# Zero-filled operands in a macaron block's attention and state-space stages: matmuls of 64 and 16 rows become matmuls of 128 rows

## The chip, the cores and the metric

One core of a Trainium2 chip runs the whole kernel. TensorE (PE) multiplies, with its weight loads shown apart (PEld); VectorE (DVE), ScalarE (ACT) and GpSimd (POOL) work beside it, and SyncE (SP) issues the weight transfers. The metric is the device time of one execution in microseconds, the median of three runs.

## The reference, cut to what matters

One layer, float32, with 16 learned meta tokens ahead of 256 positions (272 in all) and a model width of 2048:

```python
h = h + 0.5 * _swiglu(_rmsnorm(h, ffn1_norm), w_gate, w_up, w_down)      # 5632 wide
u = _rmsnorm(h, mix_norm) @ w_in                                        # q, k, v, z, x/B/C, dt
# group A: 8 heads of differential attention, two halves of 64 per head
s = einsum('bqhsd,bkhsd->bhsqk', q, k) * 64 ** -0.5;  p = softmax(where(mask, s, -inf))
w = p[:, :, 0] - lam * p[:, :, 1];  attn = rmsnorm(einsum('bhqk,bkhv->bqhv', w, v))
# group B: 16 heads of a chunked state-space scan (SSD), head size 64, state 128
h = h + concat(attn, ssd * silu(z) normed) @ w_out
h = h + 0.5 * _swiglu(_rmsnorm(h, ffn2_norm), ...);  return h[:, 16:]
```

Before the scores, q and k pass an RMS norm per half head and a rotation of the first 16 of the 64 dimensions.

## The kernel before, in words

Activations stand transposed: model dimension on the 128 partitions, positions along the row. Every weight tile (128 x 1024 float32, 512 KB) is loaded by SP, split into a high part by ACT (`hi`, L154) and a low rest by DVE (`lo`, L156), and multiplied two or three times on PE (`mm3`, L197 to L199, 272 columns; `mm2`, L204 and L205, 512 and 256 columns). These main matmuls take 128 rows and 128 columns of the array. `project` makes 4 blocks of 128 output rows from 8 weight tiles, into four of the five PSUM accumulators (`acc`); the next `project` starts in the fifth and then needs the first three of the previous one emptied.

Everything else is background work: `later(cost, fn)` puts a closure in a queue, and `step()`, called once per weight tile, runs closures worth 1.5 credits. So small float32 matmuls stand between the main ones on PE. A float32 matmul is two PE instructions (two passes); a transpose is one. The framework's scheduler fixes the final order on each engine when the program is built; at run time each engine works in order and waits on semaphores.

The matmuls that the change touches:

- `scores(h, j)`, L772: for head h and query block j, two products, one for each half s of the head. The half's 64 dimensions are rows 0 to 63 or 64 to 127 of `qT` and `kT`, so each takes 64 rows of the array; 144 columns for j = 0, 272 for j = 1. There are 16 pairs. DVE (L775 to L777), ACT (L779, L784) and DVE again (L781 to L785) make the softmax and the difference.
- `turn(h, j)`, L794 to L797: transposes the weights `w` and copies them to `wt0` or `wt1`; of the last block 16 rows are real.
- `values(h)`, L827 to L831: five products, of 128, 16, 128, 128 and 16 rows (L828 and L831 are those of 16).
- `ssd_mm(c)`, L652: for each of 8 head pairs three products per head of 128, 128 and 16 rows, 64 output rows each; the two heads of a pair take the left and the right 64 columns of the array.

Around them: `qk_evac` empties the accumulators of k (wi = 1) and q (wi = 0). For q, `join` (L226 on ACT, L227 on DVE) adds the two halves of the accumulator straight into `qT`; then ACT squares it (L676) into a row buffer and DVE scales it by the norm's weight (L677). Row buffers (`row_tmp`, tile name `t`) are 8 in all. The squares are summed by `qk_stat` (L686 on PE) in the background. `rope_in` and `rope` rotate by way of DRAM, with transfers issued by POOL (L704 to L720). `k_rows` (L745 to L755) sends k's norm factors through DRAM (`k_d`) and spreads them over the partitions; `k_scale` (L759, DVE) multiplies `kT` by them. Big activations (`qT`, `kT`, `V`, `Xd`, `O`, ...) are slots of one pool of 14 (tile name `u`).

Of the kernel before, what the change touches and what calls it, by code (L numbers as in the profile page):

```python
# [17 lines left out]
P = 128  # L18
# [66 lines left out]
def hymba_block(ctx: ExitStack, tc: tile.TileContext, h0, pars, consts, dtw, wts, out):  # L85
# [172 lines left out]
    def pc(i):  # L258
        return pcol[:, i:i + 1]
# [205 lines left out]

    brow = cp.tile([P, T], F32, name="brow")
    bcol = cp.tile([P, 3, P], F32, name="bcol")
    ends = [META - 1 + CHUNK * i for i in range(5)]

    def dt_1():  # L470
# [122 lines left out]


    Xd = Lazy([P, 1024])

    def x_step(c):
        ps = ps_tile()
# [26 lines left out]
    def ssd_exp(c):  # L625

        for h in (2 * c, 2 * c + 1):
            A = st["A"][h // 4][:, h % 4, :]

            def b(i, n, ch):  # L630
                return bcol[0:n, i, 32 * (ch - 1) + h:32 * (ch - 1) + h + 1]

            e = tmp("se", [P, 416], 4)
            for i, n, ch, o, l, k in ((0, P, 1, 0, 0, 64), (0, P, 2, 64, 64, 64), (1, P, 2, 256, 112, 16),
                                      (1, P, 3, 272, 128, 64), (1, P, 4, 336, 192, 64), (2, 16, 4, 400, 240, 16)):
                nc.vector.tensor_scalar(e[0:n, o:o + k], A[0:n, l:l + k], b(i, n, ch), 0.0, ALU.add, ALU.min)
            for ch in (3, 4):
                l = (ch - 1) * CHUNK
                nc.scalar.activation(e[:, l:l + CHUNK], A[:, l:l + CHUNK], AF.Exp, bias=b(0, P, ch))
            nc.scalar.activation(e[:, 0:P], e[:, 0:P], AF.Exp)  # L640
            nc.scalar.activation(e[:, 256:400], e[:, 256:400], AF.Exp)
            nc.scalar.activation(e[0:16, 400:416], e[0:16, 400:416], AF.Exp)
            nc.vector.tensor_tensor(e[:, 0:400], e[:, 0:400], S[h // 8][:, 0:400], ALU.mult)
            nc.vector.tensor_tensor(e[0:16, 400:416], e[0:16, 400:416], S[h // 8][0:16, 400:416], ALU.mult)
            es[h] = e

    def ssd_mm(c):
        py = ps_tile()
        for i, n, o, l in ((0, P, 0, 0), (1, P, 256, 112), (2, 16, 400, 240)):
            for j in range(2):  # L650
                h = 2 * c + j
                nc.tensor.matmul(py[j * 64:(j + 1) * 64, l:SEQ], Xd[i][0:n, h * 64:(h + 1) * 64],  # L652
                                 es[h][0:n, o:o + SEQ - l], start=i == 0, stop=i == 2)
        y = xs[c // 4][:, c % 4, META:T]
        nc.vector.scalar_tensor_tensor(y, y, dsk[:, c:c + 1], py[:, 0:SEQ], ALU.mult, ALU.add)
# [5 lines left out]
    later(0.1, lambda: (load_A(0), load_A(1)))  # L661


    kT, qT = Lazy([P, 4, T]), Lazy([P, 4, SEQ])

    def qk_evac(pj, g, dst, wi):

        sqs = []
        if wi == 0:
            for c in range(4):  # L670
                join(dst[g][:, c, :], pj[c])
            pj = [dst[g][:, c, :] for c in range(4)]
        for c in range(4):
            p = pj[c]
            sq = row_tmp(p.shape[1])
            nc.scalar.activation(sq, p, AF.Square)  # L676
            nc.vector.tensor_scalar(dst[g][:, c, :], p, pc(R_QN + wi), None, ALU.mult)  # L677
            sqs.append(sq)
        return sqs

# [18 lines left out]
    def rope_in(dst, g, n):  # L699

        d = dp.tile([2, ROT, 4, T], F32, name=nm("rope"))
        a = row_tmp(n)
        for half in range(2):
            nc.gpsimd.dma_start(d[half][:, :, 0:n], dst[g][half * HD:half * HD + ROT, :, :])  # L704
        for half in range(2):
            nc.gpsimd.dma_start(a[half * HD:(half + 1) * HD, :],
                                d[half].rearrange("r c t -> c r t")[:, :, 0:n])
        return a

    def rope(a, dst, g, t0):  # L710
        n = T - t0
        b_ = row_tmp(n)
        nc.vector.stream_shuffle(b_, a, shuf)
        nc.vector.tensor_tensor(b_, b_, sin_t[:, t0:T], ALU.mult)
        nc.vector.tensor_tensor(a, a, cos_t[:, t0:T], ALU.mult)
        nc.vector.tensor_tensor(a, a, b_, ALU.add)
        d = dp.tile([P, T], F32, name=nm("roped"))
        nc.gpsimd.dma_start(d[:, 0:n], a)
        for half in range(2):
            nc.gpsimd.dma_start(dst[g][half * HD:half * HD + ROT, :, :],  # L720
                                d[half * HD:(half + 1) * HD, 0:n].rearrange("(c r) t -> r c t", c=4))

    kst, qst = cp.tile([P, 3, 16], F32, name="kst"), cp.tile([P, 2, 16], F32, name="qst")
# [40 lines left out]
    def scores(h, j):  # L764

        kw = 144 if j == 0 else T
        w = tmp("sw", [P, 2, T], 3)
        mx, sm = tmp("mx", [P, 2]), tmp("sm", [P, 2], 3)
        pss = [ps_tile()[:, 0:kw] for _ in range(2)]
        for s in range(2):  # L770
            r = slice(s * HD, (s + 1) * HD)
            nc.tensor.matmul(pss[s], qT[h // 4][r, h % 4, j * P:(j + 1) * P], kT[h // 4][r, h % 4, 0:kw],  # L772
                             start=True, stop=True)
        for s in range(2):
            nc.vector.memset(pss[s][0:64, kw - 64:kw], -1e30)  # L775
            nc.vector.reduce_max(mx[:, s:s + 1], pss[s], axis=AX.X)
        nc.vector.scalar_tensor_tensor(mx, mx, -1.0, rq[:, j, 2 * h:2 * h + 2], ALU.mult, ALU.mult)  # L777
        for s in range(2):
            nc.scalar.activation(w[:, s, 0:kw], pss[s], AF.Exp, bias=mx[:, s:s + 1],  # L779
                                 scale=rq[:, j, 2 * h + s:2 * h + s + 1], accum_out=sm[:, s:s + 1])  # L780
        nc.vector.reciprocal(sm, sm)  # L781
        nc.vector.tensor_tensor(sm[:, 0:1], sm[:, 0:1], il, ALU.mult)
        nc.vector.tensor_tensor(sm[:, 1:2], sm[:, 1:2], nlam, ALU.mult)
        nc.scalar.activation(w[:, 1, 0:kw], w[:, 1, 0:kw], AF.Copy, scale=sm[:, 1:2])  # L784
        nc.vector.scalar_tensor_tensor(w[:, 0, 0:kw], w[:, 0, 0:kw], sm[:, 0:1], w[:, 1, 0:kw], ALU.mult, ALU.add)  # L785
        ws[h, j] = w

    def turn(h, j):
        w = ws.pop((h, j))
        pt = ps_tile()  # L790
        n = 1 + j
        t = tmp(f"wt{j}", [P, 256 + P * j])
        for i in range(n):
            nc.tensor.transpose(pt[:, i * P:(i + 1) * P], w[:, 0, i * P:(i + 1) * P], ident)  # L794
        nc.tensor.transpose(pt[0:16, n * P:(n + 1) * P], w[:, 0, n * P:n * P + 16], ident)
        nc.scalar.copy(t[:, 0:n * P], pt[:, 0:n * P])
        nc.scalar.copy(t[0:16, n * P:(n + 1) * P], pt[0:16, n * P:(n + 1) * P])  # L797
        wT[h, j] = t

    V = Lazy([P, 1024])  # L800

    def v_copy(pj):
        ts = []
# [19 lines left out]
    def values(h):  # L823
        ps = ps_tile()
        v = slice(h * P, (h + 1) * P)
        t0, t1 = wT.pop((h, 0)), wT.pop((h, 1))
        nc.tensor.matmul(ps[:, 0:P], t0[:, 0:P], V[0][:, v], start=True, stop=False)  # L827
        nc.tensor.matmul(ps[:, 0:P], t0[0:16, P:2 * P], V[1][0:16, v], start=False, stop=True)  # L828
        nc.tensor.matmul(ps[:, P:2 * P], t1[:, 0:P], V[0][:, v], start=True, stop=False)
        nc.tensor.matmul(ps[:, P:2 * P], t1[:, P:2 * P], V[1][:, v], start=False, stop=False)  # L830
        nc.tensor.matmul(ps[:, P:2 * P], t1[0:16, 2 * P:3 * P], V[2][0:16, v], start=False, stop=True)  # L831
        g, c = h // 4, h % 4
        for j in range(2):
            sq = row_tmp(P)
            nc.scalar.activation(sq, ps[:, j * P:(j + 1) * P], AF.Square, accum_out=osq[:, g, j, c:c + 1])
        nc.scalar.copy(O[g][:, :, c, :], ps[:, 0:2 * P].rearrange("p (j v) -> p j v", j=2))
# [76 lines left out]
    for c in range(8):  # L913
        later(1.2, z_b, c, label=f"z{c}")
    nc.vector.memset(kst, 1.0)
    for dst, stat, spans, t0, wi in ((kT, kst, TT, 0, 1), (qT, qst, ZT, META, 0)):
        for g in range(2):
            pj = project(t0)
            sqs = qk_evac(pj, g, dst, wi)
            a = rope_in(dst, g, T - t0)  # L920
            later(1.0, nop)
            later(0.7, lambda sqs=sqs, g=g, spans=spans, stat=stat: later_first(0.7, qk_turn, qk_stat(sqs), g, spans, stat))
            later(1.5, rope, a, dst, g, t0)
        if t0 == 0:
            later(1.0, k_rstd)
            later(0.3, nop)
            later(0.7, k_rows)
            later(1.2, k_scale, 0)
            later(1.2, k_scale, 1)
        else:  # L930
            later(1.0, head_rstd, qst, rq, (3, 4), HD ** -0.5)
    for g in range(2):
        pj = project(0)
        need("z7")
        ts = v_copy(pj)
        for c in range(4):
            later(0.0, v_turn, ts[c], 4 * g + c)
# [178 lines left out]
```

## Time and profile before

| | us |
|---|---|
| median of 3 runs (lowest, highest) | 1972.01 (1971.01, 1973.12) |
| the profiled execution's own time | 1974.47 |
| its span, first to last instruction | 1972.7 |
| granted TensorE clock over the span, share of full | 0.999 |
| PE busy / PEld / DVE / ACT / POOL | 1960.8 / 1804.7 / 1142.3 / 927.3 / 25.3 |

The span is what the trace shows; 1.8 us lie around it. A matmul's listed duration includes its way through the array, and consecutive ones overlap; what a matmul costs PE is the distance from its start to the start of the next. The timeline gives start, duration, engine, line, operation, tiles, rows*columns of the array, shape of the moving operand, and how many of the kind follow each other (x); in brackets the idle time before it and what ended it.

### The profile page before, as it was taken

To read this page: it belongs to the slowest core of one execution; us is meant where nothing else is said; L and a number is where in the kernel's file an instruction comes from. 1 tells how busy PE (TensorE), PEld (TensorE's weight loads), DVE (VectorE), ACT (ScalarE), POOL (GpSimd) and SP (SyncE) were. 2 spreads that over 40 slices of the span, in tenths; PEclk is the share of its full clock that TensorE was granted. 3 is DMA by queue.
4 is the path that set the end of the run, shared out by engine and by line. 5 is a ranking of instruction groups with operands and counts; after the bars stand their busy time and mean duration, and the time that the engine had idled before them with its cause. 6 is when DMAs were issued, how large, how long until landed. Compare 5 with 4: busy or idle time off the path is not lost.

```text
span 1972.7 us, 32522 instructions
## 1 busy us (share of the span) xinstructions
PE 1960.8 (99%) x13114; PEld 1804.7 (91%) x13114; DVE 1142.3 (58%) x1898; ACT 927.3 (47%) x1431; POOL 25.3 (1%) x61
## 2 busy tenths in 40 slices
PE   9999999999999999999999999999999999999999
PEld 9999999999999999998988878888888888888887
DVE  7554545445545456777876668565555545565554
ACT  6434343334443444456655665644444334544432
POOL 0000000000000000000011000000000000000000
PEclk9999999999999999999999999999999999999999
DMA  7555555555555555464466325556555555555563
GB/s 272 170 176 174 179 172 180 173 171 178 175 187 176 173 179 172 154 216 169 156 191 181 110 91 186 173 180 195 189 191 192 193 192 191 184 181 193 191 215 126
DMA packets 98311, 352.51 MB, mean 179 GB/s; under 512 B 11680, under 2 KB 11728, under 8 KB 98160
## 3 DMA queue, kind: packets, MB, share of 16 engines
q1 hardware_dynamic: 94464, 342.02, 52.4%
q0 software_dynamic: 2544, 6.33, 1.2%
q8 instruction: 102, 1.67, 0.3%
q10 hardware_dynamic: 1152, 2.10, 0.3%
q14 instruction: 49, 0.40, 0.1%
HBM read 347.18 MB, written 3.21 MB: 178 GB/s over the span
## 4 chain that ended last, share of the span: by engine, by line
PE 97%; DMA 1%; DVE 1%; ACT 0%; issue 0%; POOL 0%; SPq 0%; ACTq 0%; DVEq 0%
PE acc L204 22%; PE acc L198 16%; PE acc L199 16%; PE acc L197 16%; PE acc L205 11%; PE acc L1022 4%; PE acc L1021 4%; PE acc L1020 4%; PE ps L772 1%; PE ps L652 0%; DMA u<-k_d 0%; DMA raw<-in_wts_dram 0%; DVE lo L156 0%; DMA k_d<-t 0%; ACT hi L154 0%
## 5 line engine op out<-in xcount | busy, mean ns | idle before, releaser
L156 DVE TENSOR_TENSOR lo<-raw,hi 128x1024 fp32r<-128x1024 f32 x648 | 792.2, 1223 | 712.3 <-ACT hi L154 709.2
L154 ACT CAST hi<-raw 128x1024 fp32r<-128x1024 f32 x648 | 680.0, 1050 | 952.2 <-PE acc L198 457.8
L204 PE MATMUL acc<-y,hi 128*128 128x512 f32 x1664 | 584.8, 396 | 0.0
L198 PE MATMUL acc<-y,hi 128*128 128x272 f32 x1856 | 536.9, 289 | 0.0
L197 PE MATMUL acc<-y,hi 128*128 128x272 f32 x1856 | 535.2, 288 | 0.9 <-ACT hi L154 0.8
L199 PE MATMUL acc<-y,lo 128*128 128x272 f32 x1856 | 535.2, 289 | 0.5 <-DVE lo L156 0.5
L205 PE MATMUL acc<-y,lo 128*128 128x256 f32 x1664 | 466.2, 280 | 0.0
L204 PEld LDWEIGHTS acc<-y,hi 128*128 128x128 f32 x1664 | 312.6, 188 | 74.1 <-issue 0.8
L197 PEld LDWEIGHTS acc<-y,hi 128*128 128x128 f32 x1856 | 350.0, 189 | 4.0 <-issue 1.1
L199 PEld LDWEIGHTS acc<-y,lo 128*128 128x128 f32 x1856 | 349.8, 189 | 1.9 <-issue 0.7
L198 PEld LDWEIGHTS acc<-y,hi 128*128 128x128 f32 x1856 | 349.7, 188 | 1.5 <-issue 1.2
L205 PEld LDWEIGHTS acc<-y,lo 128*128 128x128 f32 x1664 | 313.5, 188 | 0.0
L199 PE MATMUL acc<-u,lo 128*128 128x272 f32 x704 | 203.9, 290 | 0.0
L197 PE MATMUL acc<-u,hi 128*128 128x272 f32 x704 | 203.4, 289 | 0.0
L198 PE MATMUL acc<-u,hi 128*128 128x272 f32 x704 | 202.6, 288 | 0.0
L1020 PE MATMUL acc<-hi,u 128*128 128x512 f32 x352 | 136.9, 389 | 0.0
L1021 PE MATMUL acc<-hi,u 128*128 128x512 f32 x352 | 136.9, 389 | 0.0
L1022 PE MATMUL acc<-lo,u 128*128 128x512 f32 x352 | 136.9, 389 | 0.0
L198 PEld LDWEIGHTS acc<-u,hi 128*128 128x128 f32 x704 | 132.9, 189 | 0.0
L199 PEld LDWEIGHTS acc<-u,lo 128*128 128x128 f32 x704 | 132.8, 189 | 0.0
L197 PEld LDWEIGHTS acc<-u,hi 128*128 128x128 f32 x704 | 132.5, 188 | 0.0
L204 PE MATMUL acc<-u,hi 128*128 128x512 f32 x256 | 94.4, 407 | 1.8 <-DVE t L227 1.8
(282 smaller groups left out, 1239.7 us busy)
## 6 DMA issues: line engine op xcount, KB each, us to landing
raw<-in_wts_dram SPq DMA_DIRECT2D x648, 512.0 KB, 3.3
u<-a_d POOLq DMA_DIRECT2D x4, 512.0 KB, 7.8
out_dram<-hx ACTq DMA_DIRECT2D x8, 256.0 KB, 4.3
hx<-in_h_dram SPq DMA_DIRECT2D x7, 272.0 KB, 7.4
u<-k_d POOLq DMA_DIRECT2D x4, 272.0 KB, 7.7
u<-in_consts_dram POOLq DMA_DIRECT2D x1, 472.0 KB, 4.8
hx<-in_h_dram SPq DMA_DIRECT2D x1, 280.0 KB, 2.8
rope<-u POOLq DMA_DIRECT2D x4, 68.0 KB, 2.5
```

The costliest lines, as they stand in the source:

```text
L154: nc.scalar.copy(hi, raw)
L156: nc.vector.tensor_tensor(lo, raw, hi.bitcast(F32), ALU.subtract)
L197: nc.tensor.matmul(ps, st_hi, mv_hi, start=first, stop=False)
L198: nc.tensor.matmul(ps, st_hi, mv_lo, start=False, stop=False)
L199: nc.tensor.matmul(ps, st_lo, mv_hi, start=False, stop=last)
L204: nc.tensor.matmul(ps, st_hi, mv, start=first, stop=False)
L205: nc.tensor.matmul(ps[:, SEQ:2 * SEQ], st_lo, mv[:, 0, :], start=False, stop=last)
L772: nc.tensor.matmul(pss[s], qT[h // 4][r, h % 4, j * P:(j + 1) * P], kT[h // 4][r, h % 4, 0:kw], start=True, stop=True)
L1020: nc.tensor.matmul(accs[j], a, hi[:, k, :], start=first, stop=False)
L1021: nc.tensor.matmul(accs[j], b_, hi[:, k, :], start=False, stop=False)
L1022: nc.tensor.matmul(accs[j], a, lo[:, k, :], start=False, stop=last)
```

## The change

Every one of the touched matmuls is given 128 rows, the added ones zero. q is kept twice, `qz0` and `qz1`, each with zeros where the other half stands, so both products of a pair read all 128 rows of `kT`. The accumulators of q are joined into row buffers (four more per half) and copied from there, half by ACT and half by DVE, into the two. `V[2]`, `Xd[2]`, the last block of the `wt` tiles and of `bcol` are zeroed by POOL, and the last matmul of each group takes all 128 rows. In `ssd_exp` the 16-row pieces of two operations fold into the wide ones.

```diff
@@ dt stage
     bcol = cp.tile([P, 3, P], F32, name="bcol")
+    nc.gpsimd.memset(bcol[:, 2, :], 0.0)
@@ SSD
     Xd = Lazy([P, 1024])
+    later(0.1, lambda: nc.gpsimd.memset(Xd[2], 0.0))
...
-                                      (1, P, 3, 272, 128, 64), (1, P, 4, 336, 192, 64), (2, 16, 4, 400, 240, 16)):
+                                      (1, P, 3, 272, 128, 64), (1, P, 4, 336, 192, 64), (2, P, 4, 400, 240, 16)):
...
-            nc.scalar.activation(e[:, 256:400], e[:, 256:400], AF.Exp)
-            nc.scalar.activation(e[0:16, 400:416], e[0:16, 400:416], AF.Exp)
-            nc.vector.tensor_tensor(e[:, 0:400], e[:, 0:400], S[h // 8][:, 0:400], ALU.mult)
-            nc.vector.tensor_tensor(e[0:16, 400:416], e[0:16, 400:416], S[h // 8][0:16, 400:416], ALU.mult)
+            nc.scalar.activation(e[:, 256:416], e[:, 256:416], AF.Exp)
+            nc.vector.tensor_tensor(e, e, S[h // 8], ALU.mult)
...
-        for i, n, o, l in ((0, P, 0, 0), (1, P, 256, 112), (2, 16, 400, 240)):
+        for i, n, o, l in ((0, P, 0, 0), (1, P, 256, 112), (2, P, 400, 240)):
@@ q and k
-    kT, qT = Lazy([P, 4, T]), Lazy([P, 4, SEQ])
+    kT = Lazy([P, 4, T])
+    qz0, qz1 = Lazy([P, 4, SEQ]), Lazy([P, 4, SEQ])
...
         if wi == 0:
+            for s in range(2):
+                nc.gpsimd.memset(dst[s][g][(1 - s) * HD:(2 - s) * HD, :, :], 0.0)
+            ts = [row_tmp(SEQ) for _ in range(4)]
             for c in range(4):
-                join(dst[g][:, c, :], pj[c])
-            pj = [dst[g][:, c, :] for c in range(4)]
+                join(ts[c], pj[c])
+            pj = ts
         for c in range(4):
...
             nc.scalar.activation(sq, p, AF.Square)
-            nc.vector.tensor_scalar(dst[g][:, c, :], p, pc(R_QN + wi), None, ALU.mult)
+            if wi == 0:
+                nc.scalar.activation(dst[0][g][0:HD, c, :], p[0:HD, :], AF.Copy, scale=pc(R_QN)[0:HD])
+                nc.vector.tensor_scalar(dst[1][g][HD:P, c, :], p[HD:P, :], pc(R_QN)[HD:P], None, ALU.mult)
+            else:
+                nc.vector.tensor_scalar(dst[0][g][:, c, :], p, pc(R_KN), None, ALU.mult)
@@ scores
-            r = slice(s * HD, (s + 1) * HD)
-            nc.tensor.matmul(pss[s], qT[h // 4][r, h % 4, j * P:(j + 1) * P], kT[h // 4][r, h % 4, 0:kw],
+            nc.tensor.matmul(pss[s], (qz0, qz1)[s][h // 4][:, h % 4, j * P:(j + 1) * P], kT[h // 4][:, h % 4, 0:kw],
                              start=True, stop=True)
@@ turn and values
+    wts_ = [[cp.tile([P, 256 + P * j], F32, name=f"wt{j}{i}") for i in range(2)] for j in range(2)]
+    for t in wts_[0] + wts_[1]:
+        nc.gpsimd.memset(t[:, -P:], 0.0)
...
-        t = tmp(f"wt{j}", [P, 256 + P * j])
+        t = wts_[j][h % 2]
...
+    def v_zero():
+        nc.gpsimd.memset(V[2], 0.0)
...
-        nc.tensor.matmul(ps[:, 0:P], t0[0:16, P:2 * P], V[1][0:16, v], start=False, stop=True)
+        nc.tensor.matmul(ps[:, 0:P], t0[:, P:2 * P], V[1][:, v], start=False, stop=True)
...
-        nc.tensor.matmul(ps[:, P:2 * P], t1[0:16, 2 * P:3 * P], V[2][0:16, v], start=False, stop=True)
+        nc.tensor.matmul(ps[:, P:2 * P], t1[:, 2 * P:3 * P], V[2][:, v], start=False, stop=True)
```

`rope_in` and `rope` read and write `dst[half][g]` instead of `dst[g]`, and `v_zero` is called once, before the first `v_copy`.

## Rows read from the trace of the kernel before

**Rows 1.** The page: the chain that ended last, by engine.

```profile
PE 97%; DMA 1%; DVE 1%; ACT 0%; issue 0%; POOL 0%; SPq 0%; ACTq 0%; DVEq 0%
```

**Rows 2.** Busy time by stretch: engines in order PE, PEld, DVE, ACT, POOL; clock.

```profile
1013.00:1066.00 53.00, 51.04 (x353) 44.88 (x352) 38.73 (x101) 23.34 (x37) 15.40 (x27) 1.00 0.73 210
1066.00:1176.00 110.00, 107.77 (x639) 86.01 (x639) 68.06 (x231) 74.30 (x230) 0.00 (x0) 1.00 0.33 108
1176.00:1182.00 6.00, 6.00 (x26) 5.17 (x27) 5.33 (x17) 1.64 (x4) 0.00 (x0) 0.72 0.01 4
```

**Rows 3.** Timeline of PE, one call of values.

```profile
1088.90 0.38 PE L827 MATMUL ps<-u,wt 128*128 128x128 f32 x2
1089.21 0.48 PE L828 MATMUL ps<-u,wt 16*128 16x128 f32 x2
1089.63 0.49 PE L829 MATMUL ps<-u,wt 128*128 128x128 f32 x2
...
1090.27 0.48 PE L831 MATMUL ps<-u,wt 16*128 16x128 f32 x2
1090.68 0.39 PE L199 MATMUL acc<-y,lo 128*128 128x272 f32 x1
1090.91 0.29 PE L197 MATMUL acc<-y,hi 128*128 128x272 f32 x1
1091.04 0.29 PE L198 MATMUL acc<-y,hi 128*128 128x272 f32 x1
```

**Rows 4.** Timeline of PE, float32 matmuls of 128 rows among their like.

```profile
1122.00 0.61 PE L306 MATMUL ps<-t,ones 128*128 128x128 f32 x4
1122.45 0.38 PE L855 MATMUL ps<-cst,u 128*128 128x128 f32 x2
...
895.77 0.59 PE L614 MATMUL ps<-u 128*128 128x256 f32 x2
896.21 0.41 PE L615 MATMUL ps<-u 128*128 128x144 f32 x2
```

**Rows 5.** Timeline of PE, single products of scores between main matmuls.

```profile
1086.88 0.28 PE L199 MATMUL acc<-y,lo 128*128 128x272 f32 x1
1087.09 0.51 PE L772 MATMUL ps<-u,u 64*128 64x144 f32 x2
...
1087.76 0.29 PE L198 MATMUL acc<-y,hi 128*128 128x272 f32 x1
...
1102.80 0.72 PE L772 MATMUL ps<-u,u 64*128 64x272 f32 x2
...
1103.68 0.29 PE L198 MATMUL acc<-y,hi 128*128 128x272 f32 x1
```

**Rows 6.** Timeline of PE, two pairs of scores that stand next to each other.

```profile
1092.71 0.73 PE L772 MATMUL ps<-u,u 64*128 64x272 f32 x4
...
1093.60 0.29 PE L197 MATMUL acc<-y,hi 128*128 128x272 f32 x1
...
1144.95 1.10 PE L772 MATMUL ps<-u,u 64*128 64x272 f32 x4
...
1146.20 0.40 PE L204 MATMUL acc<-u,hi 128*128 128x512 f32 x1
```

**Rows 7.** Timeline of PE, the last head's transposes.

```profile
1171.83 0.44 PE L794 MATMUL ps<-cst,sw 128*128 128x128 f32 x2 [0.42 <-DVE sw L785]
```

**Rows 8.** Timelines of PE and DVE where q's last statistics are taken.

```profile
1045.50 0.62 PE L686 MATMUL ps<-t,cst 128*32 128x256 f32 x2 [1.69 <-ACT t L676]
...
1043.37 1.29 DVE L759 TENSOR_TENSOR u<-u,u 128x1088 f32<-128x1088 f32 x1 [2.69 <-DMA u<-k_d]
```

**Rows 9.** Timeline of ACT, the last two squares of k's second half.

```profile
990.31 0.40 ACT L676 ACTIVATE t<-acc 128x272 f32<-128x272 f32 x1
...
1008.70 0.39 ACT L676 ACTIVATE t<-acc 128x272 f32<-128x272 f32 x1
```

**Rows 10.** Groups by line on POOL.

```profile
L517 POOL MEMSET brow<- 128x272 f32 x1 | 0.4, 357 | 0.0
```

More of the change, by code (lines that the diff above doesn't have):

```diff
@@ L703, in rope_in @@
         for half in range(2):
-            nc.gpsimd.dma_start(d[half][:, :, 0:n], dst[g][half * HD:half * HD + ROT, :, :])
+            nc.gpsimd.dma_start(d[half][:, :, 0:n], dst[half][g][half * HD:half * HD + ROT, :, :])
         for half in range(2):
@@ L719, in rope @@
         for half in range(2):
-            nc.gpsimd.dma_start(dst[g][half * HD:half * HD + ROT, :, :],
+            nc.gpsimd.dma_start(dst[half][g][half * HD:half * HD + ROT, :, :],
                                 d[half * HD:(half + 1) * HD, 0:n].rearrange("(c r) t -> r c t", c=4))
@@ L915, in hymba_block @@
     nc.vector.memset(kst, 1.0)
-    for dst, stat, spans, t0, wi in ((kT, kst, TT, 0, 1), (qT, qst, ZT, META, 0)):
+    for dst, stat, spans, t0, wi in (((kT, kT), kst, TT, 0, 1), ((qz0, qz1), qst, ZT, META, 0)):
         for g in range(2):
@@ L934, in hymba_block @@
         need("z7")
+        if g == 0:
+            v_zero()
         ts = v_copy(pj)
```

## The prediction

> **What bounds the kernel now.** The page's chain of work that ended last comes first: 97% of it is PE, and no other engine has more than 1% [rows 1]. So what PE is spared in the middle of its stream ends the program earlier by as much, unless PE then waits. Second, the busy time by stretch: in the attention stage (1066 to 1176 us) PE is busy for 107.8 of 110 us, DVE for 68.1 and ACT for 74.3 [rows 2], so neither of those two bounds it. PE's busy share hides the loss in question, though, because a late matmul counts as busy while it passes through the array. Third, then, the PE timeline, read from start to start. Main matmuls of 272 columns follow each other by 0.13 us (1090.91, 1091.04). The five products of a head's values, ten passes, take from 1088.90 to 1090.68, and the first main matmul after them still has a step of 0.23 us to the next [rows 3]. What the reader is to see: wherever the number of rows goes from 128 to 16 or back, the step is 0.2 us in place of 0.11, and once more after it.
>
> **Values.** The like without a change of rows is there too: four float32 passes of 128 rows and 128 columns take 1122.00 to 1122.45, 0.111 us each; two passes of 256 columns 895.77 to 896.21, 0.22 each [rows 4]. With ten passes of 0.111 and a main step of 0.126, the stretch from 1088.90 to 1090.91 (2.01 us) would take 1.24. That spares 0.77 us a head, four changes of 0.19 each; 8 heads, **6.2 us**. There is little to bound here: the passes keep their columns, and zeros are data like any other.
>
> **Scores.** A pass of 144 columns is interpolated between the two measured sizes, 0.124 us; one of 272 is 0.229 by the same line (an estimate from [rows 4]). A single product of 144 columns between main matmuls: 1086.88 to 1087.76, 0.88 us, where 0.126 + 2 x 0.124 + 0.126 = 0.50 would do: 0.38 spared. One of 272: 1102.80 to 1103.68 is 0.88, and the late start before it is 0.085 (1086.88 to 1087.09 in place of 0.126); against 0.46 + 0.126, 0.38 again [rows 5]. In the PE timeline of 1073 to 1166 us 22 products, eleven of the sixteen pairs, stand singly like this: 22 x 0.385 = **8.5 us**. The other five pairs stand next to each other, and their price differs. In the one at 1092.71 both halves run at once, in rows 0 to 63 and 64 to 127: 0.89 + 0.085 before, 4 x 0.229 + 0.126 = 1.04 after, a loss of 0.07. The one at 1144.95 runs in sequence: 1.25 + 0.085 before, a gain of 0.30 [rows 6]. The five lie between, three of them near 0.1 to 0.3; I take 0.15 each, **0.75 us** (bounds -0.35 and 1.5).
>
> [...]
>
> **SSD.** The last piece changes from 16 to 128 rows, at the same 64 columns of the array, so of the changes around a group only the one inside it goes. One change of rows is worth 0.19 us where the stream goes on behind it, as in the values; here the other column width follows, whose change stays. I take half, 8 x 0.1 = **0.8 us** (bounds 0 and 1.5).
>
> Sum on PE: 6.2 + 8.5 + 0.75 + 0.8 = 16.25 us.
>
> **What doesn't reach the end.** The last head's second half is not covered: PE waits 0.42 us at its transposes for DVE's L785 [rows 7], the end of the softmax of the scores of 1165.5. The values of head 6 lie between those scores and these transposes, so their 0.77 us only lengthens the wait. Left: 15.5 us. The rest of the stage's 2.2 us of idle PE [rows 2], 1.8, follows head 7's own values, while ACT and DVE empty an accumulator; that work starts when these values end, so their 0.77 us count. The clock falls to 0.72 on average right behind these waits [rows 2]; they stay, so I leave it there.
>
> **Around q.** What q's path gets is eight ACT copies of 64 rows more, each like a square of 0.40 us, 3.2 us in a stretch where ACT is busy for 23.3 of 53 us [rows 2]; DVE's scalings keep their number and length. That is hidden, but the order is tight here. PE waits 1.69 us at L686 for a square that waits for a join, which stands on DVE behind L759, which waits 2.69 us for k's factors from DRAM [rows 8]. The four new row buffers per half come from the same eight: k's fourth square already started 18.4 us after its third (990.31, 1008.70) [rows 9], as no buffer was free. A join that waits so delays either PE's next projection or k's own chain through L759. Bounds: the 1.69 us vanish if the join goes ahead of L759 (gain 1.7), or grow by what k's chain is late (up to 7, below). Nearest is what stands there now, a wait of the same length with a little more ahead of it: **-1.0 us**.
>
> **Edits at nothing.** POOL's zeroing: 272 columns took 0.36 us [rows 10], so 1024 take about 1.3, six of these, and five small ones, 9 us in all, on an engine that is busy for 15.4 of 53 us around q and idle in the attention stage [rows 2]. If one is queued ahead of a rotation's transfer it costs that transfer 1.3 to 2.6 us, which has until the first scores at 1073. Two slots more of the 14: with mc, four of z, two of kT, four of q, and three of V, 14 are held at most, so none should wait; if one did, `O` would, and with it the values, by the time to the next free slot, a weight tile or two (2.8 us each). The 32 small operations less in `ssd_exp` ran under PE.
>
> 15.5 - 1.0 = 14.5 us. The profiled execution would take 1974.5 - 14.5 = 1960.0, and the median, which lies 2.5 lower, 1972.0 - 14.5 = **1957.5 us**.
>
> **Rivals.** Under 0.2% (3.9 us) counts as no change, about what a measurement of this kernel can tell.
>
> Row buffers: the joins of q take the buffers that k's sums and rotation need, and k's chain (L686, statistics, `k_d`, L759) comes later by 2 to 7 us, one to two and a half weight tiles of 2.8 us. L686 passes it on one to one: 1959.5 to 1964.5. For it speaks the square that waited [rows 9]; against it, that PE's sums L686, which free four buffers at once, don't need one.
>
> [...]
>
> Nothing: the late step belongs to the change of operands or from one float format to the other, not to the rows. Then only the format remains and the time is 1972 within 2. Against it, L306 and L614 change these too and start on time [rows 4].
>
> Slower: the second or third join of q's first half waits for a row buffer as long as k's square did, 18.4 us. PE's next projection needs those accumulators from its second block on, has a few us of other work, and stands still; from a wait of 14.5 us more than now the kernel is no faster, and at 18.4 it is 3.9 slower, 1976. For it, the row of that square [rows 9]; against it, PE's L686 came only because PE was busy with other queued work.
>
> **How the numbers follow.** Forecast 0.68, with its own range 1954 to 1961 (the bounds of pairs and SSD, -1.8 to +1.5; L686 gone, -2.7; a little more waiting). Row buffers 0.17, packing 0.04, nothing 0.06, slower 0.05. Faster: 0.68 + 0.17 + 0.04 = 0.89. From 1953.5 to 1965 lie nearly all of the first three but their tails, 0.83.
>
> **What would show it.** In the PE timeline L772's successor has steps of 0.12 to 0.13 again, with 0.25 or 0.46 from a single product's start to the next main matmul; a head's values take 1.1 us, and all their forms read 128 rows. The stretch from the first scores to the last values gets shorter by some 14 us. Wrong would be: steps of 0.2 after float32 products of 128 rows; an idle time at L686 or at L204 of over 4 us around 1013 to 1045; idle time of PE at L794 for L785 in more heads than the last.

## The result, and the profile after

The changed kernel takes 1959.05 us (median of six, 1956.69 to 1961.24) where the kernel before, beside it, takes 1972.57 (median of six, 1971.01 to 1973.79): ratio 0.9925, 95% interval 0.9915 to 0.9934. Forecast were 1957.5, range 1953.5 to 1965. The two profiled executions are further apart than the medians: 1974.47 before, 1959.02 after, 15.45 us; what follows places those 15.45.

The chain that ended last, from the page of the changed kernel, is PE's still, one per cent more than before [rows 1]:

```profile
PE 98%; DVE 1%; ACT 0%; DMA 0%; issue 0%; SPq 0%; ACTq 0%
```

Since PE carries the end, one can number its main matmuls (those into `acc`) from 0 and compare when the same one starts in both traces:

| main matmul | before, us | after, us | earlier by | what lies behind it |
|---|---|---|---|---|
| 7200th | 937.0 | 936.6 | 0.41 | FFN1 and the start, which no edit touches |
| 7600th | 999.3 | 997.5 | 1.81 | SSD: 1.40 |
| 7800th | 1038.7 | 1036.9 | 1.77 | k and q's first half: nothing |
| 8000th | 1067.6 | 1064.2 | 3.38 | q's second half: 1.61 |
| 8400th | 1175.8 | 1160.4 | 15.45 | attention: 12.07 |
| last | 1968.1 | 1952.7 | 15.45 | the rest: nothing |

From the 8000th to the 8400th, PE's instructions stand in the same order in both kernels, so this stage compares like with like. Around q the order differs.

Now the rows. Busy time by stretch, in the columns of [rows 2]; the second stretch starts at the same 1066 us, when the changed kernel is 3.4 us further on in its work, and ends at the first main matmul behind the last values:

```profile
1013.00:1066.00 53.00, 52.78 (x370) 46.83 (x369) 40.24 (x99) 28.06 (x50) 17.70 (x30) 1.00 0.75 222
1066.00:1160.40 94.40, 91.35 (x611) 81.37 (x610) 66.91 (x230) 71.24 (x225) 0.00 (x0) 1.00 0.36 119
1160.40:1166.40 6.00, 6.00 (x25) 5.22 (x26) 5.34 (x17) 1.64 (x4) 0.00 (x0) 0.72 0.01 3
```

Around q, PE has hardly any idle time left (52.78 of 53 us; 51.04 before). ACT is busy for 4.7 us more there and POOL for 2.3, both far from full. The clock behind the attention is 0.72, as before.

PE's timeline, one call of values, beside [rows 3]:

```profile
1083.21 0.39 PE L843 MATMUL ps<-u,wt 128*128 128x128 f32 x2
1083.44 0.39 PE L844 MATMUL ps<-u,wt 128*128 128x128 f32 x2
1083.66 0.39 PE L845 MATMUL ps<-u,wt 128*128 128x128 f32 x2
...
1084.11 0.39 PE L847 MATMUL ps<-u,wt 128*128 128x128 f32 x2
1084.25 0.37 PE L199 MATMUL acc<-y,lo 128*128 128x272 f32 x1
1084.46 0.28 PE L197 MATMUL acc<-y,hi 128*128 128x272 f32 x1
```

Every product now starts 0.22 to 0.23 after the one ahead of it (two passes of 0.11). From the first to the second main matmul behind it are 1.25 us (1083.21 to 1084.46) where before there were 2.01, as forecast (1.24).

PE's timeline, one pair of scores standing singly, beside [rows 5]:

```profile
1081.83 0.29 PE L199 MATMUL acc<-y,lo 128*128 128x272 f32 x1
1081.99 0.51 PE L780 MATMUL ps<-u,u 128*128 128x144 f32 x2
1082.25 0.39 PE L197 MATMUL acc<-y,hi 128*128 128x272 f32 x1
1082.47 0.29 PE L198 MATMUL acc<-y,hi 128*128 128x272 f32 x1
1082.60 0.29 PE L199 MATMUL acc<-y,lo 128*128 128x272 f32 x1
1082.72 0.41 PE L780 MATMUL ps<-u,u 128*128 128x144 f32 x2
1082.87 0.38 PE L197 MATMUL acc<-y,hi 128*128 128x272 f32 x1
1083.09 0.29 PE L198 MATMUL acc<-y,hi 128*128 128x272 f32 x1
```

The second product is what the forecast had for all: 0.12 after the main matmul, 0.37 from its start to the second main one. The first is not: it starts 0.16 after its forerunner, its own passes take 0.51 where the other's take 0.41, and from 1081.83 to the second main matmul behind it are 0.64 (1082.47) where the other takes 0.49 (1082.60 to 1083.09). The list of waits says what it waits for; PE's weight loads in the attention stage, by line, with what they waited for (us in total, times, longest):

```profile
PEld ps L780 <- ACT sw L787: 1.3, 6, 0.3
...
PEld ps L845 <- ACT wt L809: 0.2, 1, 0.2
```

L787 is ACT's exponential. There are three PSUM tiles `ps`, and a pair takes two, so by this list the first product of a pair needs a tile that the exponential of the pair before still reads. In the trace before, the same wait of L772 for L779 stands in the list with 1.5 us in six, under steps that were late anyway.

Last, PE's timeline at the end of the attention, beside [rows 7]:

```profile
1156.68 0.44 PE L807 MATMUL ps<-cst,sw 128*128 128x128 f32 x2 [1.18 <-DVE sw L793]
...
1157.07 0.39 PE L843 MATMUL ps<-u,wt 128*128 128x128 f32 x2
1157.29 0.39 PE L844 MATMUL ps<-u,wt 128*128 128x128 f32 x2
1157.69 0.49 PE L845 MATMUL ps<-u,wt 128*128 128x128 f32 x2
...
1160.40 0.50 PE L204 MATMUL acc<-u,hi 128*128 128x512 f32 x1 [1.78 <-DVE t L227]
```

The wait at the last transposes grew from 0.42 to 1.18 us, by 0.76, which is what head 6's values were spared. And from the second to the third product of the last head's values it takes 0.40 and not 0.22 (1157.29 to 1157.69).

### The profile page after: what moved, and what is told of

Its sections match the earlier page's. It is cut to its first block, busy times and chain, and to the rows that moved or that the text cites. A ratio compares the mean times of both kernels' runs of the same rounds, so it can differ in the third digit from the quotient of the medians.

```text
span 1957.2 us, 32523 instructions
## 1 busy us (share of the span) xinstructions
PE 1945.9 (99%) x13114; PEld 1803.2 (92%) x13114; DVE 1142.6 (58%) x1882; ACT 927.4 (47%) x1423; POOL 31.6 (2%) x72
## 4 chain that ended last, share of the span: by engine, by line
PE 98%; DVE 1%; ACT 0%; DMA 0%; issue 0%; SPq 0%; ACTq 0%
PE acc L204 23%; PE acc L198 16%; PE acc L199 16%; PE acc L197 16%; PE acc L205 11%; PE acc L1040 4%; PE acc L1038 4%; PE acc L1039 4%; PE ps L780 1%; PE ps L652 0%; DMA raw<-in_wts_dram 0%; DVE lo L156 0%; ACT hi L154 0%; PE ps L1008 0%; PE ps L807 0%
```

## The experiments

**The three parts one by one.** Each puts one part of the change into the kernel before.

```diff
 values alone
-        nc.tensor.matmul(ps[:, 0:P], t0[0:16, P:2 * P], V[1][0:16, v], start=False, stop=True)
+        nc.tensor.matmul(ps[:, 0:P], t0[:, P:2 * P], V[1][:, v], start=False, stop=True)
...
 scores alone (and q's row buffers and two copies)
-            nc.tensor.matmul(pss[s], qT[h // 4][r, h % 4, j * P:(j + 1) * P], kT[h // 4][r, h % 4, 0:kw],
+            nc.tensor.matmul(pss[s], (qz0, qz1)[s][h // 4][:, h % 4, j * P:(j + 1) * P], kT[h // 4][:, h % 4, 0:kw],
...
 SSD alone
-        for i, n, o, l in ((0, P, 0, 0), (1, P, 256, 112), (2, 16, 400, 240)):
+        for i, n, o, l in ((0, P, 0, 0), (1, P, 256, 112), (2, P, 400, 240)):
```

Values: 

> The kernel before with the values alone at 128 rows (zeros in V[2] and in the last block of the wt tiles). Theory (each change of the number of rows on PE costs about 0.19 us): a head's ten passes take 1.1 us in place of 1.8, 6.0 to 6.2 us less in all; of these 0.77 comes back as a longer wait of PE at the last head's transposes (0.42 to about 1.2 us), so 5.3 us less than before, about 1967.3. Rival, the late starts belong to the operands or formats and not to the rows: no difference. Rival, the whole gain of the changed kernel comes from another order of work around q: no difference here either.

Scores: 

> The kernel before with the scores alone at 128 rows (q kept twice with zeros, joined by way of row buffers). Theory: 7.7 us less in the scores' stretch, as the trace of the changed kernel shows, and 1.6 us less if PE's wait at the statistics of q's second half goes here as it did there: 7.5 to 9.5 us less, 1963 to 1965. If all of each late start had belonged to the rows, as the prediction had it: 9.25 us in that stretch. Rival, the row buffers delay k's chain: the wait at these statistics is longer than 1.7 us and the time above 1966.

SSD: 

> The kernel before with the SSD's last piece alone at 128 rows. Theory: a group of twelve passes takes 0.14 to 0.15 us less, eight groups 1.2 us; the prediction had 0.8. In the time that is 1971.4 against 1972.6, too little for one look; it is read from the trace. Rival, the change of the columns of the array hides the change of rows: 0.

Against 1974.11 (median of 17 on that chip), values alone take 1968.32 (ratio 0.9968, 0.9957 to 0.9979), scores alone 1964.96 (0.9951, 0.9936 to 0.9966), and SSD alone, one execution, 1974.17. The first two are 5.8 and 9.1 us, and both traces show a part of it elsewhere: around q, 0.9 and 1.5 us, since PE's wait of 1.69 us at the statistics [rows 8] is 0.8 in the one and gone in the other. Values alone add only one zeroing on POOL there (0.97 us), and the order on PE, DVE and ACT is that of the kernel before, so their 0.9 us are most likely scatter of a single execution. In the attention stage the same main matmul comes 4.3 and 7.9 us earlier; together that is 12.2, where the whole change has 12.07.

SSD alone, PE's timeline, one block of twelve products with the two main matmuls behind it (in the kernel before the same block starts at 942.07 and its second main matmul at 943.35, 1.28 us):

```profile
941.47 0.97 PE L652 MATMUL ps<-se,u 128*64 128x256 f32 x12
942.38 0.39 PE L197 MATMUL acc<-y,hi 128*128 128x272 f32 x1
942.61 0.28 PE L198 MATMUL acc<-y,hi 128*128 128x272 f32 x1
```

1.14 us, 0.14 spared; over the six blocks of twelve and one of 24 it is 1.26. Hardly any of it reaches the time of this run: its wait at the statistics is 2.5 us and not 1.69, in the same order of instructions, and from the 8200th to the 8400th main matmul, at the end of the attention, it loses 1.5 more, while the granted clock is 0.50 (1163 to 1165 us).

**A change of rows fewer.** The kernel before, with the second group of a head's values in another order, so that the two 16-row products stand together:

```diff
-        nc.tensor.matmul(ps[:, P:2 * P], t1[:, 0:P], V[0][:, v], start=True, stop=False)
-        nc.tensor.matmul(ps[:, P:2 * P], t1[:, P:2 * P], V[1][:, v], start=False, stop=False)
-        nc.tensor.matmul(ps[:, P:2 * P], t1[0:16, 2 * P:3 * P], V[2][0:16, v], start=False, stop=True)
+        nc.tensor.matmul(ps[:, P:2 * P], t1[0:16, 2 * P:3 * P], V[2][0:16, v], start=True, stop=False)
+        nc.tensor.matmul(ps[:, P:2 * P], t1[:, 0:P], V[0][:, v], start=False, stop=False)
+        nc.tensor.matmul(ps[:, P:2 * P], t1[:, P:2 * P], V[1][:, v], start=False, stop=True)
```

> The kernel before with nothing padded: of a head's values only the order changes, 128, 16, 16, 128, 128 rows in place of 128, 16, 128, 128, 16. Theory (the change of rows costs, not their number): two changes a head in place of four, 16 x 0.19 = 3.1 us less, of which 0.4 comes back at the last head: 2.7 us less, about 1969.9; a head's passes take 1.4 us in place of 1.8. Rival, a matmul of few rows is slow by itself and zeros are what helps: no difference, 1.8 us a head.

PE's timeline of it:

```profile
1091.05 0.38 PE L827 MATMUL ps<-u,wt 128*128 128x128 f32 x2
1091.36 0.48 PE L828 MATMUL ps<-u,wt 16*128 16x128 f32 x2
1091.68 0.38 PE L829 MATMUL ps<-u,wt 16*128 16x128 f32 x2
1091.99 0.49 PE L830 MATMUL ps<-u,wt 128*128 128x128 f32 x2
...
1092.46 0.37 PE L199 MATMUL acc<-y,lo 128*128 128x272 f32 x1
1092.67 0.29 PE L197 MATMUL acc<-y,hi 128*128 128x272 f32 x1
```

1.62 us to the second main matmul, in place of 2.01 with four changes and 1.25 with none: each change costs 0.19, with nothing zero-filled. The whole kernel takes 1972.82 (ratio 0.999, 0.9979 to 1.0001), 1.3 us less than the kernel before by the medians, which isn't clear of the noise, and the 2.7 us expected do not show. In the profiled execution two things take them away. The attention stage gets 1.7 us shorter and not 2.7, mostly since two of the eight heads gain nothing: the one whose ten passes main matmuls interrupt keeps its four changes, and in the last one the third product comes late. And the wait at the statistics, where the order is that of the kernel before, is 2.3 us, with a granted clock of 0.81 after it (1043 to 1052 us), so the 8000th main matmul starts 2.1 later than before.

**64 rows in place of 16.** The kernel before with 64-row operands (48 rows zero) for the 16-row products of the values:

```diff
-        nc.tensor.matmul(ps[:, 0:P], t0[0:16, P:2 * P], V[1][0:16, v], start=False, stop=True)
+        nc.tensor.matmul(ps[:, 0:P], t0[0:64, P:2 * P], V[1][0:64, v], start=False, stop=True)
...
-        nc.tensor.matmul(ps[:, P:2 * P], t1[0:16, 2 * P:3 * P], V[2][0:16, v], start=False, stop=True)
+        nc.tensor.matmul(ps[:, P:2 * P], t1[0:64, 2 * P:3 * P], V[2][0:64, v], start=False, stop=True)
```

> The kernel before, with the values' last products (V[1] of the first block, V[2] of the second) at 64 rows, 48 of them zero, in place of 16; everything else as before. If what costs is that the number of rows changes at all, four changes a head stay and a head's ten passes take as long as before, 1.8 us from the first to the first main matmul after them, 0.77 us over their like of 128 rows. If the price grows with how far the row counts lie apart, 64 beside 128 costs about half: 1.4 us. If only very small matmuls are dear, 1.1 us. To be read from the PE timeline; the time itself should stay near 1974.

PE's timeline of it:

```profile
1090.36 0.38 PE L834 MATMUL ps<-u,wt 128*128 128x128 f32 x2
1090.67 0.48 PE L835 MATMUL ps<-u,wt 64*128 64x128 f32 x2
1091.09 0.49 PE L836 MATMUL ps<-u,wt 128*128 128x128 f32 x2
...
1092.14 0.39 PE L199 MATMUL acc<-y,lo 128*128 128x272 f32 x1
1092.38 0.29 PE L197 MATMUL acc<-y,hi 128*128 128x272 f32 x1
```

From the first product to the second main matmul it is 2.02 us, what [rows 3] has with 16 rows (2.01), step by step; the time of this single execution, 1974.56, is within that of the kernel before (1971.69 to 1974.87). Between 16 and 64 rows, then, the number makes no difference: what costs is that it changes. A change costs 0.19 us here, and 16-row products in a row cost nothing on top (above, 1.62 us with two changes, 2.01 with four); what PE does in that time, no run shows.

**q's row buffers alone.** The kernel before, with q joined into row buffers and scaled from there into `qT`:

```diff
+            ts = [row_tmp(SEQ) for _ in range(4)]
             for c in range(4):
-                join(dst[g][:, c, :], pj[c])
-            pj = [dst[g][:, c, :] for c in range(4)]
+                join(ts[c], pj[c])
+            pj = ts
```

> The kernel before, with q's accumulators joined into four row buffers per half and squared and scaled from there into qT, as the changed kernel does it; no second copy of q, no more rows anywhere. If the row buffers alone let the scheduler put a weight tile's cast and ten main matmuls between the statistics products, PE's wait there (1.69 us in the kernel before, 2.3 to 2.5 in two of the single edits) goes, the q stage is 1 to 2 us shorter, and the profiled execution takes about 1973. The rival: it is ACT's part of q's scaling, eight copies of 64 rows, that moves the order; then the wait stays between 0.8 and 2.5 us. A second rival, as forecast: the joins wait for row buffers and the wait grows to over 3 us.

DVE's timeline, and below it PE's, of this kernel:

```profile
1041.94 0.42 DVE L227 TENSOR_TENSOR t<-acc,t 128x256 f32<-128x256 f32 x1
1042.61 1.29 DVE L760 TENSOR_TENSOR u<-u,u 128x1088 f32<-128x1088 f32 x1 [0.25 <-DMA u<-k_d]
```

```profile
1043.09 0.64 PE L687 MATMUL ps<-t,cst 128*32 128x256 f32 x8
```

In [rows 8] the fourth join stood on DVE behind the multiplication that waits for `k_d`; here it stands ahead of it, and all eight statistics passes run without a break. The wait of 1.69 us is gone, and PE, 0.2 us ahead at the 7800th main matmul, is 2.4 ahead at the 8000th. The single execution took 1969.87. At the last main matmul it is 4.6 us ahead; 1.8 of that came just behind the attention, where its clock did not fall (granted clock 1.00 from 1160 to 1182 us; 0.72 in the last row of [rows 2]).

How far to trust a single execution here, all the traces together say. From the 7800th to the 8000th main matmul the five that keep the old code around q take 28.0 to 31.1 us (the kernel before 28.9), with the same order of instructions on PE, DVE and ACT. The seven that have the new code, also in one order, take 27.3 to 28.2, and the row buffers alone 26.7. So the new code is faster there, by about 2 us between the middle values, but the 1.6 us that the pair of profiles gives is not known to a microsecond.

**One PSUM tile for a pair.** The changed kernel, with the two products of 144 columns in one tile:

```diff
-        pss = [ps_tile()[:, 0:kw] for _ in range(2)]
+        if j == 0:
+            one = ps_tile()
+            pss = [one[:, s * kw:(s + 1) * kw] for s in range(2)]
+        else:
+            pss = [ps_tile()[:, 0:kw] for _ in range(2)]
```

> The changed kernel, but the two products of a first query block (2 x 144 columns) lie in one PSUM tile, so that such a pair needs one of the three tiles and not two. If the scores fell short of their term because a pair's first product waits until ACT has read the pair before, the late starts of first products at 144 columns (six of 0.10 to 0.24 us, 1.08 us in all) go, and the time is 1.0 to 1.5 us below the changed kernel's. The rival: the lateness belongs to the operands or to PE's order; then the same six starts stay late and the time is the same. A third way: DVE and ACT read one half of the tile while PE writes the other and must now wait for it, and the time is 1 to 3 us above.

Beside it ran the changed kernel itself: 

> The changed kernel again, unaltered, on the chip of the three runs beside it, to compare them with: 12 to 17 us under the kernel before (ratio 0.9915 to 0.9934 as first measured).

The changed kernel takes 1958.53 there (1957.65 to 1961.25; ratio 0.993, 0.9914 to 0.9947), the one with the shared tile 1955.80 (1955.19 to 1957.26; 0.9913, 0.9898 to 0.9928): 2.7 us less by the medians. The intervals of the two ratios overlap, but the highest of the shared tile's four times is below the lowest of the changed kernel's four. PE's timeline of the shared tile:

```profile
1083.31 0.66 PE L784 MATMUL ps<-u,u 128*128 128x144 f32 x4
1083.80 0.38 PE L847 MATMUL ps<-u,wt 128*128 128x128 f32 x2
...
1148.31 0.62 PE L784 MATMUL ps<-u,u 128*128 128x272 f32 x2
...
1155.05 0.38 PE L811 MATMUL ps<-cst,sw 128*128 128x128 f32 x2
```

The pair runs through in 0.49 us, four passes of 0.12, and the six waits for the exponential are gone from the list of waits. But the edit did more than free a tile. It changed PE's order in the attention stage too: about half of its instructions there stand elsewhere, and all eight pairs of 144 columns stand together now, six of them right behind transposes. So the run doesn't tell the free tile from the new order, which was its rival. The gain at the scores is half of what was expected, 0.5 us over all pairs, as products of 272 columns, which still take a tile each, now come up to 0.28 us late (one of 0.16: from 1079.07 to the second main matmul 0.87 us, where 0.71 would do). The larger part stands at the end: the last scores start 6.7 us ahead of the last transposes (1148.31, 1155.05; in the changed kernel 6.4, with the wait), and PE no longer waits there, 1.18 us. From the 8000th to the 8400th main matmul both together and 0.6 us that I did not place make 2.3.

**More background work per tile.** The changed kernel, 2.0 credits per step in place of 1.5 from the second half of the output projection until the last head is needed; then the same with the shared tile, and with 1.75:

```diff
-        credit[0] = min(credit[0] + STEP, 2 * STEP)
+        credit[0] = min(credit[0] + more[0], 2 * more[0])
...
+    more[0] = 2.0
...
     need("o7")
+    more[0] = STEP
```

2.0: 

> The changed kernel with 2.0 in place of 1.5 credits of background work per weight tile from the second half of the output projection until the point that needs the last attention head. If the tail of the attention (PE's waits of 1.18 us at the last transposes and of 1.78 us at the accumulator, and the low-clock stretch behind them, about 1.2 us more) stands there only because the background work is spread too thin, the last head is done while main matmuls are left to cover it, and up to 4 us go: about 1955 where the changed kernel has 1959. The rival: the chain of one head (softmax on ACT and DVE, transposes, values, norm) is what the end waits for, whatever the rate; then the same waits stay within 0.5 us and the time is the same within 1 us.

2.0 and the shared tile: 

> The changed kernel with the one PSUM tile for a first query block's pair and with 2.0 credits per weight tile from the second half of the output projection on. With 2.0 credits alone the end's waits of 1.18 and 1.78 us turned into five of 0.3 to 0.5 us, several of them for a PSUM tile that ACT still reads. If these came from the three tiles, the shared tile takes away two or three of them, and the time is 1 to 2 us under that of the shared tile alone (ratio to the kernel before 0.9913), about 1954. The rival: the softmax chain of a head sets the pace at that rate, the waits stay, and the time is that of the shared tile alone or up to 1 us above.

1.75 and the shared tile: 

> The same with 1.75 credits. Between the two rates: if the end is a matter of the rate alone, the wait of 1.78 us behind the last values gets main matmuls to cover it while the softmax has more time than at 2.0, and this is the fastest of the four, 1953 to 1954.5; if the chain of a head sets the pace, it is the same as the shared tile alone within 1 us.

They take 1959.12 (ratio 0.9929, 0.9914 to 0.9944), 1960.70 (0.9933, 0.9917 to 0.995) and 1961.20 (0.9938, 0.9924 to 0.9953): the first like the changed kernel, the other two some 5 us above the shared tile alone (4 to 5 by the ratios, since they ran on another chip). PE's waits in the attention stage, at 2.0, and below that at 2.0 with the shared tile:

```profile
PE ps L809 <- DVE sw L795: 0.5, 1, 0.5
PE ps L782 <- ACT u L854: 0.5, 1, 0.5
PE ps L782 <- ACT wt L812: 0.5, 1, 0.5
PE ps L782 <- ACT sw L789: 0.4, 1, 0.4
PE acc L206 <- DVE t L229: 0.3, 1, 0.3
```

```profile
PE ps L813 <- DVE sw L799: 2.3, 1, 2.3
PE acc L206 <- DVE t L229: 0.8, 1, 0.8
```

The two waits of the end (1.18 and 1.78) do turn into smaller ones at 2.0, but they stand further up now: PE waits for the softmax of the pair ahead, with the shared tile in one place for 2.3 us. None of the three expectations was right in full. The waits did not stay, as the rivals had it, nor did the time fall; for 2.0 alone it stayed the same within 1 us, which was the rival's time. At a higher rate PE meets a head's chain through ACT and DVE earlier. That is not all of the 5 us, though. In the profiled executions the way from the 8000th to the 8600th main matmul is 5.4 us longer at 2.0 than with the shared tile alone, part of it under a granted clock of 0.50 (1146 to 1149 us), and at 1.75 only 2.4 us longer. About 1.8 us more were lost in both near the start, where nothing was edited and the granted clock is 0.50 (13 to 15 us; 1.00 in the runs that they are compared with), and at 1.75 another 2.4 us behind the 8800th main matmul, where nothing was edited either. How much of the medians the rate explains stays open.

## Why the forecast held, point by point

The gain was forecast as 14.5 us in the profiled execution and came to 15.45; for the medians 14.5 were forecast and 13.5 came (14.7 on the chip of the second comparison). The median lies 1.55 us above the forecast, although the profiled execution gained more, because I took 2.5 us off the profiled execution for the way it stood to the median before; the profile after stands at its median.

- **Values, forecast 6.2.** That a change of rows is what costs, and its price of 0.19 us, hold, also by the order with two changes and by the 64 rows. Six heads give 0.77 us each. Two give less: the last one 0.31 (from its first product to the next main matmul, 3.64 before, 3.33 after), and the one at 1100.86, whose passes a main matmul interrupts, 0.61. The sum is 5.5. The failed step is "that work starts when these values end, so their 0.77 us count": the last head's third product now waits for the second block's transposed weights (the 0.40 above), so faster passes only reach that wait sooner. That ACT's copy is what is late is by the list of waits, not by an experiment.
- **Scores, forecast 9.25.** This is the mis-sized term: counted as in the forecast, all products together cost 9.6 us above their like before and 1.85 after, a gain of 7.75. Missing are late starts, most of them of first products. The forecast saw to the change of rows and took for granted that whatever else a product needs is there. That the missing thing is a free PSUM tile stands in the list of waits for the six first products of 144 columns, 1.08 us in all. The shared tile took these waits away, but with another order of PE, so that it fits this cause and does not prove it; it returned only half, as products of 272 columns then came late.
- **SSD, forecast 0.8.** It came to 1.26, 0.16 a head pair: most of a change's 0.19 and not half, so the other column width behind it covers little.
- **The tail, forecast -0.77.** It came to -0.76, at the place named, and to -0.75 with values alone (0.42 to 1.17).
- **Around q, forecast -1.0.** It came to +1.6 in this pair of profiles, and to between 0.7 and 1.6 in the others with the same code, against the same profile before. The failed step is "Nearest is what stands there now, a wait of the same length with a little more ahead of it". The bound at the other end, the wait gone, came nearly true, by another order of instructions, and the row buffers alone bring it. In the changed kernel the join still stands behind the multiplication by k's factors, but ACT's and DVE's work on the next weight tile stands ahead of both, and PE has main matmuls between the statistics: PE's timeline there,

```profile
1041.40 0.76 PE L695 MATMUL ps<-t,cst 128*32 128x256 f32 x6
1042.09 0.39 PE L197 MATMUL acc<-y,hi 128*128 128x272 f32 x1
...
1043.55 0.62 PE L695 MATMUL ps<-t,cst 128*32 128x256 f32 x2
```

- **The rivals.** Row buffers: in this profile PE has no wait of 0.3 us or more around q (with the same code 0.28 and 0.87 in two others), and k's chain was not late: its transfer to `k_d` is issued at 1028.1 us in place of 1030.1. q's joins didn't stand still either: ACT's first four squares of q end at 1019.0 us, and at 1019.6 before. The row that spoke for this rival, k's fourth square [rows 9], does not show a missing buffer: ACT comes to it straight from a weight tile's cast (1007.75 us), one of six that stand between the two squares, so it is late by its place in ACT's order. Why the scheduler put it there stays open. Packing, that a single pair would cost what pairs do that stand together: the pairs stayed single, and ran at the forecast's price where nothing was missing (0.49 us from 1082.60 to 1083.09, forecast 0.50). The rivals "nothing" and "slower" are ruled out by the steps above and by the time.

In the attention stage 5.5 + 7.75 - 0.76 make 12.5, where the trace has 12.07; 0.4 are not placed, nor are the 0.41 from the start, which no edit touches. So the cause, the change of rows, was right, but the total came this near by luck, as the errors of its terms cancelled: 2.2 too much in values and scores, 3.1 too little in SSD and around q.

## What to carry to other kernels

Here a lone matmul of 16 rows between matmuls of 128 cost 0.19 us at each of its edges, and one of 64 rows as much (2.01 and 2.02 us for a head's values): give such a one the full rows with zeros (1.25 us), or put the odd ones next to each other, which saved half of the price on PE without any zeros (1.62 us). Before counting on the whole price, look at what the next instruction needs anyway (a free PSUM tile, a copied operand), since here such waits showed once the other price was gone: up to 0.24 us at the first product of a pair, and 0.40 us in place of 0.22 from the second to the third product of the last head's values. And an edit that adds or shares buffers can change the order in which a scheduler places operations: around q that was worth about 2 us, more than the gain in SSD, and in the run with the shared tile it spoils the proof. Compare the order of instructions before you call a difference the edit's. Where the order was the same, the stage around q still differed by up to 3 us between executions.

## What the runs showed of the hardware that was not expected

The clock behind the same wait is not the same in each execution. The changed kernel was profiled twice with the same 1.78 us of idle PE at the accumulator at the end of the attention. In the first the granted clock was 0.50 from 1161.30 to 1164.30 us, in the second it was 1.00; busy time by stretch, the first and the second execution:

```profile
1161.30:1164.30 3.00, 3.00 (x11) 2.51 (x10) 2.87 (x11) 0.55 (x1) 0.00 (x0) 0.50 0.03 5
```

```profile
1161.30:1164.30 3.00, 3.00 (x18) 2.58 (x18) 3.00 (x12) 1.05 (x1) 0.00 (x0) 1.00 0.02 5
```

The 8400th main matmul starts at 1160.4 in both, the 8600th at 1198.2 and 1196.8: 1.4 us of scatter from this place alone. Likewise a wait of 2.3 us at the statistics was followed by a granted clock of 0.81 on average (1043 to 1052 us, with the values' order changed), one of 2.5 us by 1.00 (the same stretch, with SSD alone), and a shorter one of 1.62 us by 0.50 (1047 to 1049 us, with 64 rows). A forecast to within a microsecond is not to be had for such a kernel from one profile.
